# Feed forward products of a two-block transformer on block matrices: seven block products in place of eight for gate with up, and for the down projection of 16 of 22 f tiles

## The chip, the core and the metric

The kernel runs on one core of a Trainium2 chip. The metric is the device time of one execution in microseconds. A core has five engines with instruction queues of their own: TensorE (PE in the rows; its weight loads are PEld), VectorE (DVE), ScalarE (ACT), GpSimd (POOL) and SyncE (SP), which here issues nearly all DMA transfers. SBUF and PSUM are the memories on the core, each of 128 partitions; matmuls write PSUM alone, in banks of 128 x 512 float32 values.

## What is computed

Two transformer blocks follow each other on 512 tokens of width 1024, in float32. Each block has attention, or a mixer, and then a gated feed forward, with D_FF = 2816 = 22 tiles of 128. The change concerns the feed forwards alone:

```python
h = rms_norm(x, norm_ffn_pre[l])                                              # first block
f = (jax.nn.silu(h @ w_gate[l]) * (h @ w_up[l])) @ w_down[l]
x = x + rms_norm(f, norm_ffn_post[l])
...
h = rms_norm_2(x, norm_ffn[i])                                                # second block
x = x + (jax.nn.silu(h @ w_ffn_gate[i]) * (h @ w_ffn_up[i])) @ w_ffn_down[i]
```

## The kernel before, in words

**Precision.** Every large product is made of three matmuls (`mm3`, L136): a float32 operand is kept as a high part, rounded to float32r by ScalarE, and a low part, the rest, made by VectorE (or POOL). The products are high x high, high x low and low x high, summed in one PSUM bank. `load_w` (L123) loads 128 x 1024 weights by SyncE into a `raw` buffer (L131), ScalarE writes the high part (L132), `pl["lo"]` the low part (L133), into a `wt` buffer. `split_from` (L222) does the same for values on the core (L225, L226). Low parts of this kind read two operands from SBUF.

**The feed forward** (`ffn`, L664, called at L724 and L1022) goes over the 22 f tiles in three runs, 6, 8 and 8 (`SPLITS`). For each f tile `glu` (L653) makes gate and up with `t_mm` (L195): the weights stand in TensorE, all 512 tokens of the transposed input `hT` move, 8 k tiles x 3 matmuls for each. In the first run the first four tiles (`NFIRST`) are made in two halves of 256 tokens, so that the work begins when half of the tokens are ready. ScalarE makes the silu (L660), VectorE multiplies with up from PSUM (L661), and the result is split: high part on ScalarE (L225), low part on POOL (L226). Then the run's down products, `n_mm` (L202): for each of four token tiles two banks of 512 columns. VectorE adds them to a running result (L707, L709; L1011 in the second block), and after the last run the norms and transposes for the next part follow (`evac1`, `evac2`). All low parts of weights are VectorE's in these runs; eight weights of the head are POOL's.

**Before it**, in the first block, `norm_fill` (L589) makes the norm of a token tile and `tr_fill` (L596) transposes it (`transpose_tile`, L169); tiles 2 and 3 are made as late as inside the feed forward. In the second block the input comes tile by tile from the output projection.

**What sets the order.** The tile framework places instructions by priority and data, puts the semaphores in, and takes buffers from pools: 21 buffers `u`, two `raw`, four `wt1` and more `wt` in a phase, and eight PSUM banks (three `acc`, two `f`, one `av`, two `tp`). A load waits until its buffer is free, and engines work through their queues in order.

## Time and profile before

| | us |
|---|---|
| median of 3 runs | 1373.46 (1372.19 to 1374.2) |
| the profiled execution | 1375.31 |
| its span, first to last instruction | 1373.5 |
| TensorE busy | 1324.0 (96%) |
| VectorE busy | 715.1 (52%) |
| ScalarE busy | 595.1 (43%) |
| POOL busy | 250.2 (18%) |
| mean granted TensorE clock | 0.988 of full |

The page gives busy time of each engine, the span in 40 slices, the chain of work that ended last, groups of equal instructions and DMA issues. Ends of matmuls are modelled, so the distance from start to start tells their pace, not their listed duration. A duration on VectorE or POOL holds what the instruction waited for inside the engine; waits for semaphores are listed as idle time before it.

### The profile page before, as it was taken

The numbers are of one execution on the slowest core, as the hardware profiler recorded it, in microseconds if no ns is written. First come the engines' busy times: TensorE is split into PE (matmuls) and PEld (weight loads), VectorE is DVE, ScalarE is ACT, GpSimd is POOL, SyncE is SP. The second block draws the span as 40 slices with busy tenths as digits, with TensorE's granted clock in tenths as the row PEclk, the third lists the DMA queues.
The fourth block names the chain that finished last, engine by engine and source line by source line (L and its number), as shares of the span: only waits on it lengthen the run. The fifth ranks groups of instructions, "written<-read, shape, count | busy, mean of one in ns | idle before, by whom it ended". The sixth has DMA issues, their size and how long they took to land.

```text
span 1373.5 us, 17214 instructions
## 1 busy us (share of the span) xinstructions
PE 1324.0 (96%) x6476; PEld 1080.8 (79%) x6476; DVE 715.1 (52%) x1399; ACT 595.1 (43%) x1087; POOL 250.2 (18%) x255
## 2 busy tenths in 40 slices
PE   8889998899999999999999999989999999999997
PEld 6656666798888888878777778879988888888886
DVE  5889677742433242386886672655423321422464
ACT  5578876340322132244866564524413220422252
POOL 1433234320111011100323010115210110021002
PEclk9999999899999999999999999999999999999999
DMA  7212123241533143223121435634424330532031
GB/s 271 92 31 78 47 74 111 93 138 47 153 92 107 39 146 98 71 93 100 63 77 54 130 132 192 198 108 143 134 77 121 95 106 17 160 115 93 1 108 62
DMA packets 44771, 139.64 MB, mean 102 GB/s; under 512 B 7312, under 2 KB 7696, under 8 KB 44688
## 3 DMA queue, kind: packets, MB, share of 16 engines
q1 hardware_dynamic: 44544, 138.54, 31.8%
q8 instruction: 51, 0.84, 0.2%
q14 instruction: 32, 0.26, 0.1%
q10 hardware_dynamic: 144, 0.00, 0.0%
HBM read 130.14 MB, written 8.39 MB: 101 GB/s over the span
## 4 chain that ended last, share of the span: by engine, by line
PE 76%; DVE 9%; issue 7%; ACT 3%; POOL 2%; DMA 1%; POOLq 0%; ACTq 0%; DVEq 0%
PE acc L139 10%; PE acc L140 10%; PE acc L138 10%; PE f L140 10%; PE f L138 10%; PE f L139 10%; PE av L139 3%; PE av L138 3%; PE av L140 3%; DVE wt L133 2%; PE av L475 1%; DVE p L858 1%; PE tp L468 1%; DMA raw<-in_w_out 1%; PE tp L175 1%
## 5 line engine op out<-in xcount | busy, mean ns | idle before, releaser
L133 DVE TENSOR_TENSOR wt<-raw,wt 128x1024 fp32r<-128x1024 f32 (+1 forms) x204 | 254.2, 1247 | 280.8 <-ACT wt L132 279.8
L132 ACT ACTIVATE wt<-raw 128x1024 fp32r<-128x1024 f32 (+1 forms) x220 | 231.3, 1056 | 352.4 <-issue 84.2
L138 PE MATMUL f<-u,wt 128*128 128x512 f32 (+1 forms) x556 | 210.8, 379 | 4.3 <-DVE u L575 4.1
L139 PE MATMUL f<-u,wt 128*128 128x512 f32 (+1 forms) x556 | 210.0, 378 | 0.2 <-DVE u L218 0.2
L140 PE MATMUL f<-u,wt 128*128 128x512 f32 (+1 forms) x556 | 209.6, 377 | 0.0
L226 POOL TENSOR_TENSOR u<-t,u 128x512 fp32r<-128x512 f32 (+1 forms) x52 | 82.1, 1580 | 541.0 <-ACT u L225 541.0
L139 PE MATMUL acc<-u,wt 128*128 128x512 f32 (+1 forms) x432 | 155.0, 359 | 0.0
L138 PE MATMUL acc<-u,wt 128*128 128x512 f32 (+1 forms) x432 | 154.9, 359 | 0.0
L140 PE MATMUL acc<-u,wt 128*128 128x512 f32 (+1 forms) x432 | 154.8, 358 | 0.0
L138 PEld LDWEIGHTS f<-u,wt 128*128 128x128 f32 x556 | 106.3, 191 | 23.1 <-DVE u L575 4.3
L138 PE MATMUL f<-wt,u 128*128 128x512 f32 x302 | 120.6, 399 | 2.1 <-ACT u L225 2.1
L140 PE MATMUL f<-wt,u 128*128 128x512 f32 x302 | 119.9, 397 | 1.4 <-DVE u L226 1.4
L139 PEld LDWEIGHTS f<-u,wt 128*128 128x128 f32 x556 | 106.4, 191 | 17.1 <-DVE u L218 0.4
L140 PEld LDWEIGHTS f<-u,wt 128*128 128x128 f32 x556 | 106.4, 191 | 16.9
L139 PE MATMUL f<-wt,u 128*128 128x512 f32 x302 | 119.4, 396 | 0.0
L138 PE MATMUL acc<-wt,u 128*128 128x512 f32 (+1 forms) x288 | 112.7, 391 | 5.9 <-ACT wt L132 5.9
L139 PE MATMUL acc<-wt,u 128*128 128x512 f32 (+1 forms) x288 | 112.8, 392 | 1.6 <-DVE wt L133 1.5
L140 PE MATMUL acc<-wt,u 128*128 128x512 f32 (+1 forms) x288 | 112.4, 390 | 0.0
L138 PEld LDWEIGHTS acc<-u,wt 128*128 128x128 f32 x432 | 82.2, 190 | 12.0
L140 PEld LDWEIGHTS acc<-u,wt 128*128 128x128 f32 x432 | 82.0, 190 | 11.9
L139 PEld LDWEIGHTS acc<-u,wt 128*128 128x128 f32 x432 | 82.0, 190 | 11.8
L661 DVE TENSOR_TENSOR t<-t,acc 128x512 f32<-128x512 f32 (+1 forms) x52 | 31.4, 604 | 94.4 <-PE acc L140 91.3
(257 smaller groups left out, 2138.0 us busy)
## 6 DMA issues: line engine op xcount, KB each, us to landing
raw<-in_w_out SPq DMA_DIRECT2D x24, 512.0 KB, 3.7
raw<-in_w_gate SPq DMA_DIRECT2D x22, 512.0 KB, 3.6
raw<-in_w_up SPq DMA_DIRECT2D x22, 512.0 KB, 3.6
raw<-in_w_down SPq DMA_DIRECT2D x22, 512.0 KB, 3.6
raw<-in_w_ffn_gate SPq DMA_DIRECT2D x22, 512.0 KB, 3.5
raw<-in_w_ffn_up SPq DMA_DIRECT2D x22, 512.0 KB, 3.5
raw<-in_w_ffn_down SPq DMA_DIRECT2D x22, 512.0 KB, 3.5
raw<-in_w_in SPq DMA_DIRECT2D x11, 512.0 KB, 5.5
```

Of the source, the lines that this page charges most:

```text
L132: nc.scalar.activation(w[:, 0, c], raw[:, c], AF.Copy)
L133: pl["lo"].tensor_tensor(w[:, 1, c], raw[:, c], w[:, 0, c].bitcast(F32), op=ALU.subtract)
L138: nc.tensor.matmul(ps, lhsT=st[0], rhs=mv[0], start=first, stop=False)
L139: nc.tensor.matmul(ps, lhsT=st[0], rhs=mv[1], start=False, stop=False)
L140: nc.tensor.matmul(ps, lhsT=st[1], rhs=mv[0], start=False, stop=last)
L175: nc.tensor.transpose(pt[:, j * P:(j + 1) * P], h_t[:, k * P:(k + 1) * P], ident)
L226: (lo_eng or nc.vector).tensor_tensor(lo, src, hi.bitcast(F32), op=ALU.subtract)
L468: nc.tensor.transpose(pt[:, c:c + P], pn[j][:, kc * P:(kc + 1) * P], ident)
L475: nc.tensor.matmul(o[s * 64:s * 64 + 64], lhsT=VT[kc][:, kv], rhs=ts[s][:, i * 256:i * 256 + 256], start=kc == 0, stop=kc == NT - 1, skip_ ...
L661: nc.vector.tensor_tensor(s[:, :n], s[:, :n], pu[:, :n], op=ALU.mult)
L858: nc.vector.tensor_tensor_scan(c[:, n - 1::-1], ones.to_broadcast([P, n]) if nq == 1 else restart[:, :n], e[:, n - 1::-1], 0.0, op0=ALU.mu ...
```

## The change

A matrix product of 2 x 2 blocks is made with seven block products, of sums and differences of the blocks, in place of eight.

*Gate and up together.* The left matrix is h, cut into two halves of 256 tokens and two of 512 inputs; the right one is [gate, up] of an f tile, cut the same way by inputs. The seven left blocks (`a11`, `a12`, `a22`, `p1`, `s2`, `s3`, `p4`) are made once by transposing h and differences of its halves (`left_raw`, `left_rest`). The right ones are the raw blocks and four sums for each f tile (`sums`), made by POOL from the raw weights and split by ScalarE and VectorE. Each of the seven products (`prod`) has 4 k tiles x 3 matmuls of 256 columns. VectorE combines them out of PSUM (`glu`).

*Down* for f tiles 0 to 15, in four groups of four: `down_left` makes the left blocks by POOL subtractions, `down_weights` the sums of two pairs of weight tiles, `down7` seven products of 12 matmuls of 512 columns and the sums onto the running result, by VectorE and POOL. The last six f tiles are done as before.

*Around it.* The head makes the gate's two raw products of six f tiles (`glu_head`, `NFIRST = 6`), whose raw weights are loaded again for the sums. Raw weights come through three buffers, split weights through five `wt` buffers and `u`, sums through three `e` buffers. x of the first block is written to memory before the feed forward and read again after it. Down weights lie as 22 tiles of 128 x 1024.

```diff
-NFIRST = 4
+NFIRST = 6
...
+    def sums(b11, b12, b21, b22):
+        e = pl["e"]
+        ta, tb = (e.tile([P, 2, 512], F32, tag="e", name=nm("e")) for _ in range(2))
+        add = nc.gpsimd.tensor_tensor
+        add(ta[:, 0], b11, b12, op=ALU.add)
+        add(tb[:, 0], ta[:, 0], b22, op=ALU.add)
+        add(tb[:, 1], b12, b22, op=ALU.add)
+        wb = w8(flat(tb))
+        add(ta[:, 1], tb[:, 0], b21, op=ALU.add)
+        wa = w8(flat(ta))
+        return wb, wa
...
+    def left_rest(X, h0, h1, j):
+        c1, c2 = u_tile([P, 2, 512]), u_tile([P, 2, 512])
+        sub = nc.vector.tensor_tensor
+        sub(c1[:, 0], h1[:, 0:512], h1[:, 512:1024], op=ALU.subtract)
+        sub(c1[:, 1], h0[:, 0:512], c1[:, 0], op=ALU.subtract)
+        left_block(X, "s2", c1[:, 1], j)
+        sub(c2[:, 0], h0[:, 0:512], h1[:, 0:512], op=ALU.subtract)
+        left_block(X, "s3", c2[:, 0], j)
+        left_block(X, "p1", c1[:, 0], j)
+        left_block(X, "a22", h1[:, 512:1024], j)
+        sub(c2[:, 1], h0[:, 512:1024], c1[:, 1], op=ALU.subtract)
+        left_block(X, "p4", c2[:, 1], j)
...
+    def glu_head(X, E, wg, f):
+        G = load_raw(wg[f])
+        w = w8(G)
+        ps = any8()
+        prod(ps, w, 0, X["a11"], True)
+        nc.scalar.activation(E[:, 0], ps[:, :256], AF.Copy)
+        prod(ps, w, 512, X["a12"], False)
+        silu(E[:, 2], ps[:, :256])
+    def glu(X, E, wg, wu, f, dst):
+        h = slice(0, 256)
+        tt = nc.vector.tensor_tensor
+        G, Uw = load_raw(wg[f]), load_raw(wu[f])
+        head = E is not None
+        if not head:
+            E = pl["ee"].tile([P, 4, 256], F32, tag="ee", name=nm("ee"))
+            wG = w8(G)
+        wb, wa = sums(G[:, 0:512], Uw[:, 0:512], G[:, 512:1024], Uw[:, 512:1024])
+        w22 = w4(Uw[:, 512:1024])
+        if not head:
+            pp = any8()
+            prod(pp, wG, 0, X["a11"], True)
+            nc.scalar.activation(E[:, 0], pp[:, h], AF.Copy)
+        up = t_tile([P, 2, 256])
+        pn = any8()
+        prod(pn, wb, 0, X["s2"], True)
+        tt(E[:, 1], pn[:, h], E[:, 0], op=ALU.subtract)
+        pq = any8()
+        prod(pq, wb, 512, X["s3"], True)
+        tt(up[:, 1], E[:, 1], pq[:, h], op=ALU.subtract)
+        pr = any8()
+        prod(pr, wa, 0, X["p1"], True)
+        tt(up[:, 1], pr[:, h], up[:, 1], op=ALU.add)
+        prod(pq, wa, 512, X["a22"], False)
+        tt(E[:, 3], pq[:, h], E[:, 1], op=ALU.subtract)
+        silu(E[:, 3], E[:, 3])
+        if not head:
+            prod(pp, wG, 512, X["a12"], False)
+            silu(E[:, 2], pp[:, h])
+        prod(pr, w22, 0, X["p4"], False)
+        tt(up[:, 0], pr[:, h], E[:, 1], op=ALU.add)
+        tt(dst, E[:, 2:4].rearrange("p a b -> p (a b)"), flat(up), op=ALU.mult)
...
+    def down_left(ra, last):
+        rb = u_tile([P, 4, 256])
+        sub = nc.gpsimd.tensor_tensor
+        sub(rb[:, 0], ra[:, 1], ra[:, 3], op=ALU.subtract)
+        sub(rb[:, 1], ra[:, 0], rb[:, 0], op=ALU.subtract)
+        sub(rb[:, 2], ra[:, 0], ra[:, 1], op=ALU.subtract)
+        sub(rb[:, 3], ra[:, 2], rb[:, 1], op=ALU.subtract)
+        T = [u_tile([P, 2, 2, 256], F32R) for _ in range(3)]
+        t0 = last if last is not None else u_tile([P, 2, 2, 256], F32R)
+        i0 = 0 if last is None else 1
+        split_from(ra[:, 0], t0[:, 0, i0], t0[:, 1, i0])
+        for t, src in ((T[0], flat(ra[:, 2:4])), (T[1], flat(rb[:, 0:2])), (T[2], flat(rb[:, 2:4]))):
...
+    def down_weights(wdown, f1, f2):
+        K1, K2 = load_raw(wdown[f1]), load_raw(wdown[f2])
+        w11 = w4(K1[:, 0:512])
+        wb, wa = sums(K1[:, 0:512], K1[:, 512:1024], K2[:, 0:512], K2[:, 512:1024])
+        return dict(b11=(w11, 0), t2=(wb, 0), t3=(wb, 512), t1=(wa, 0), t4=(wa, 512)), K2
...
+    def down7(wdown, fs, left, acc, fresh):
+        n = len(left)
+        W, K2 = zip(*[down_weights(wdown, fs[i], fs[n + i]) for i in range(n)])
+        tt = nc.vector.tensor_tensor
+        pt = nc.gpsimd.tensor_tensor
+        lo, hi = slice(0, 512), slice(512, 1024)
+        def product(banks, x, b, first):
+            for j in range(2):
+                for i in range(n):
+                    t, a = left[i][x]
+                    w, off = W[i][b]
+                    st = (t[:, 0, a, j * P:(j + 1) * P], t[:, 1, a, j * P:(j + 1) * P])
+                    mv = wcols(w, off, off + 512)
+                    for m, (u, v) in enumerate(((0, 0), (0, 1), (1, 0))):
+                        nc.tensor.matmul(banks[j], lhsT=st[u], rhs=mv[v], start=first and i == 0 and m == 0,
+                                         stop=i == n - 1 and m == 2, skip_group_check=True)
...
+        bq = [any8() for _ in range(2)]
+        product(bq, "s3", "t3", True)
+        wv = [t_tile([P, 512]) for _ in range(2)]
+        for j in range(2):
+            tt(wv[j], v[j], bq[j], op=ALU.subtract)
+            if not fresh:
+                pt(acc[2 + j][:, hi], acc[2 + j][:, hi], wv[j], op=ALU.add)
+                pt(acc[2 + j][:, lo], acc[2 + j][:, lo], v[j], op=ALU.subtract)
+                pt(acc[j][:, hi], acc[j][:, hi], v[j], op=ALU.add)
...
+        for i in range(n):
+            w2 = w8(K2[i])
+            W[i].update(b21=(w2, 0), b22=(w2, 512))
...
+        for n in GROUPS:
+            fs, left, last = list(range(f0, f0 + n)), [], None
+            for i in range(n // 2):
+                ra = u_tile([P, 4, 256])
+                for half, f in ((0, fs[i]), (1, fs[n // 2 + i])):
+                    glu(X, heads.get(f), wgate, wup, f, flat(ra[:, 2 * half:2 * half + 2]))
+                    if i == 0 and half == 0:
+                        release()
+                last, names = down_left(ra, last if i % 2 else None)
+                left.append(names)
+            held.append((fs, left))
+            f0 += n
...
-    def glu(hT, wg, wu, gt, halves):
-        for c0, c1 in halves:
-            n = c1 - c0
-            pg, pu = any_tile(), any_tile()
-            t_mm(pg, wg, 0, hT, c0, c1)
-            t_mm(pu, wu, 0, hT, c0, c1)
-            s = t_tile([P, S])
-            silus.append(nc.scalar.activation(s[:, :n], pg[:, :n], AF.Silu))
-            nc.vector.tensor_tensor(s[:, :n], s[:, :n], pu[:, :n], op=ALU.mult)
-            split_from(s[:, :n], gt[:, 0, c0:c1], gt[:, 1, c0:c1], lo_eng=nc.gpsimd)
```

What stands in the queues, in two places of the first feed forward.

POOL, f tiles 6 to 13, of the kernel before (`u` the split product, `t` the product):

```order
L226 TENSOR_TENSOR u_3686<-t_3754,u_3686 128x512
L226 TENSOR_TENSOR u_3687<-t_3819,u_3687 128x512
L226 TENSOR_TENSOR u_3688<-t_3884,u_3688 128x512
L226 TENSOR_TENSOR u_3689<-t_3949,u_3689 128x512
L226 TENSOR_TENSOR u_3690<-t_4014,u_3690 128x512
L226 TENSOR_TENSOR u_3691<-t_4079,u_3691 128x512
L226 TENSOR_TENSOR u_3692<-t_4144,u_3692 128x512
L226 TENSOR_TENSOR u_3693<-t_4209,u_3693 128x512
```

and of the changed kernel, from the sums of f tile 8 to those of the first down weights (`e` a sum, `raw` a raw weight, `u` left blocks of the down products):

```order
L270 TENSOR_TENSOR e_4148<-raw_4140,raw_4142 128x512
L272 TENSOR_TENSOR e_4149<-raw_4142 128x512
L271 TENSOR_TENSOR e_4149<-e_4148,raw_4142 128x512
L274 TENSOR_TENSOR e_4148<-e_4149,raw_4140 128x512
L385 TENSOR_TENSOR u_4123<-u_3911 128x256
L270 TENSOR_TENSOR e_4268<-raw_4261 128x512
L272 TENSOR_TENSOR e_4269<-raw_4261,raw_4263 128x512
L271 TENSOR_TENSOR e_4269<-e_4268,raw_4263 128x512
L274 TENSOR_TENSOR e_4268<-e_4269,raw_4263 128x512
L383 TENSOR_TENSOR u_4123<-u_3911 128x256
L384 TENSOR_TENSOR u_4123<-u_3911,u_4123 128x256
L386 TENSOR_TENSOR u_4123<-u_3911,u_4123 128x256
```

In the place of one low part for each f tile stand four additions, and subtractions and the sums of down weights among them.

VectorE, from f tile 14 on, of the kernel before (`wt` a weight's low part, `t` the product with up):

```order
L709 TENSOR_TENSOR u_3683<-acc_4435,u_3683 128x512
L133 TENSOR_TENSOR wt_4606<-raw_4605,wt_4606 128x1024
L133 TENSOR_TENSOR wt_4666<-raw_4665,wt_4666 128x1024
L133 TENSOR_TENSOR wt_4671<-raw_4670,wt_4671 128x1024
L661 TENSOR_TENSOR t_4530<-t_4530,acc_4481 128x512
L133 TENSOR_TENSOR wt_4731<-raw_4730,wt_4731 128x1024
L133 TENSOR_TENSOR wt_4736<-raw_4735,wt_4736 128x1024
L133 TENSOR_TENSOR wt_4796<-raw_4795,wt_4796 128x1024
L661 TENSOR_TENSOR t_4595<-t_4595,acc_4546 128x512
L133 TENSOR_TENSOR wt_4801<-raw_4800,wt_4801 128x1024
L133 TENSOR_TENSOR wt_4861<-raw_4860,wt_4861 128x1024
```

and of the changed kernel, about the end of f tile 7 (`ee` and `t` partial results, tiles from `acc`, `tp`, `av` in PSUM):

```order
L377 TENSOR_TENSOR u_3911<-ee_4006,t_4039 128x512
L226 TENSOR_TENSOR wt_4273<-e_4269,wt_4273 128x1024
L226 TENSOR_TENSOR wt_4277<-e_4268,wt_4277 128x1024
L226 TENSOR_TENSOR u_4128<-u_3911,u_4128 128x512
L226 TENSOR_TENSOR u_4129<-u_4123,u_4129 128x512
L226 TENSOR_TENSOR u_4130<-u_4123,u_4130 128x512
L226 TENSOR_TENSOR u_4160<-raw_4142,u_4160 128x512
L362 TENSOR_TENSOR ee_4144<-acc_4178,ee_4144 128x256
L365 TENSOR_TENSOR t_4177<-ee_4144,tp_4192 128x256
L368 TENSOR_TENSOR t_4177<-acc_4206,t_4177 128x256
L370 TENSOR_TENSOR ee_4144<-tp_4192,ee_4144 128x256
L376 TENSOR_TENSOR t_4177<-acc_4206,ee_4144 128x256
```

Low parts of weights stood between single products; now three low parts, the combinations that wait for TensorE's products, and the splits of left blocks follow each other in one queue.

## Rows read from the trace of the kernel before

**Rows 1.** The page: span, busy time of each engine, shares of the last chain.
```profile
span 1373.5 us, 17214 instructions
PE 1324.0 (96%) x6476; PEld 1080.8 (79%) x6476; DVE 715.1 (52%) x1399; ACT 595.1 (43%) x1087; POOL 250.2 (18%) x255
...
PE 76%; DVE 9%; issue 7%; ACT 3%; POOL 2%; DMA 1%; POOLq 0%; ACTq 0%; DVEq 0%
```

**Rows 2.** Windows of 100 us: length, busy us of each engine, clock, DMA.
```profile
300.00:400.00 100.00, 100.00 (x443) 82.80 (x442) 34.45 (x34) 27.96 (x33) 10.35 (x6) 1.00 0.34 103
400.00:500.00 100.00, 100.00 (x443) 82.81 (x442) 31.44 (x31) 23.21 (x27) 8.53 (x5) 1.00 0.30 91
1000.00:1100.00 100.00, 100.00 (x443) 82.68 (x442) 31.55 (x32) 25.29 (x30) 10.87 (x6) 1.00 0.32 99
1100.00:1200.00 100.00, 100.00 (x443) 82.81 (x442) 31.41 (x32) 24.23 (x29) 8.51 (x5) 1.00 0.30 91
```

**Rows 3.** Timeline, TensorE, first feed forward: start, us, engine, line, operation.
```profile
329.70 0.39 PE L140 MATMUL acc<-wt,u 128*128 128x512 f32 x1
...
374.12 0.39 PE L138 MATMUL f<-u,wt 128*128 128x512 f32 x1
```

**Rows 4.** Timeline, TensorE: first row of each stage, first after it.
```profile
231.22 0.28 PE L138 MATMUL acc<-u,wt 128*128 128x256 f32 x1
...
611.92 0.39 PE L138 MATMUL f<-wt,u 128*128 128x512 f32 x1
...
944.20 0.36 PE L138 MATMUL f<-u,wt 128*128 128x256 f32 x1
...
1308.64 0.27 PE L175 MATMUL tp<-ident,u 128*128 128x128 f32 x1
```

**Rows 5.** Timeline, TensorE, start of the second feed forward.
```profile
943.41 1.03 PE L175 MATMUL tp<-ident,u 128*128 128x128 f32 x8
...
944.40 0.28 PE L139 MATMUL f<-u,wt 128*128 128x256 f32 x1
...
946.20 0.28 PE L139 MATMUL f<-u,wt 128*128 128x256 f32 x1
```

**Rows 6.** Groups on POOL: shapes, count | busy us, mean ns | idle before.
```profile
L1052 POOL TENSOR_TENSOR u<-u,row 128x512 f32<-128x512 f32 x7 | 9.0, 1292 | 87.1 <-DVE u L1050 82.9 <-issue 4.2
L1052 POOL TENSOR_TENSOR u<-u,row 128x256 f32<-128x256 f32 x2 | 1.5, 734 | 2.9 <-DVE u L1050 2.9
```

**Rows 7.** Timeline, VectorE and POOL where they meet, and POOL alone (405.07).
```profile
361.50 1.23 DVE L133 TENSOR_TENSOR wt<-raw,wt 128x1024 fp32r<-128x1024 f32 x1 [0.70 <-ACT wt L132]
362.07 1.82 POOL L226 TENSOR_TENSOR u<-t,u 128x512 fp32r<-128x512 f32 x1 [42.75 <-ACT u L225]
...
405.07 1.28 POOL L226 TENSOR_TENSOR u<-t,u 128x512 fp32r<-128x512 f32 x1 [8.86 <-ACT u L225]
...
893.56 1.29 POOL L970 TENSOR_TENSOR t<-t,u 128x512 f32<-128x512 f32 x1 [2.77 <-ACT t L967]
893.85 2.08 DVE L133 TENSOR_TENSOR wt<-raw,wt 128x1024 fp32r<-128x1024 f32 x1
...
935.75 2.44 DVE L155 SCALAR_TENSOR_TENSOR rs_t<-rs_y,rs_a 128x1 f32<-128x1 f32 x1
935.76 4.75 POOL L133 TENSOR_TENSOR wt<-raw,wt 128x1024 fp32r<-128x1024 f32 x2 [29.78 <-ACT wt L132]
938.31 2.22 DVE L159 SCALAR_TENSOR_TENSOR rs_y<-rs_t,rs_y 128x1 f32<-128x1 f32 x1
...
942.89 2.40 POOL L133 TENSOR_TENSOR wt<-raw,wt 128x1024 fp32r<-128x1024 f32 x1 [2.38 <-DMA u<-spill_x]
943.05 0.69 DVE L988 TENSOR_TENSOR u<-f,u 128x512 f32<-128x512 f32 x1 [0.99 <-DMA u<-spill_x]
943.66 0.68 DVE L988 TENSOR_TENSOR u<-acc,u 128x512 f32<-128x512 f32 x1
```

**Rows 8.** Groups on VectorE by shape: two SBUF inputs, and one from PSUM (L661).
```profile
L317 DVE TENSOR_TENSOR t<-t,t 128x512 f32<-128x512 f32 x8 | 5.5, 687 | 1.2 <-POOL t L314 1.0
L420 DVE TENSOR_TENSOR sq<-sq,sq 128x256 f32<-128x256 f32 x10 | 4.6, 460 | 1.4 <-ACT sq L417 1.4
L661 DVE TENSOR_TENSOR t<-t,acc 128x256 f32<-128x256 f32 x16 | 6.7, 417 | 12.6 <-PE acc L140 9.6 <-ACT t L660 2.9
```

**Rows 9.** Timeline, VectorE: the last step of the norms in the first stage.
```profile
262.87 1.89 DVE L1070 SCALAR_TENSOR_TENSOR u<-x,rs_y,row 128x512 f32<-128x512 f32 x2
```

**Rows 10.** The page, DMA issues: transfers, KB each, us to landing.
```profile
raw<-in_w_up SPq DMA_DIRECT2D x22, 512.0 KB, 3.6
```

**Rows 11.** Groups on ScalarE: the high parts.
```profile
L132 ACT ACTIVATE wt<-raw 128x1024 fp32r<-128x1024 f32 x217 | 229.5, 1062 | 351.9 <-issue 84.2 <-PE f L140 70.9 <-PE acc L140 49.2
L225 ACT ACTIVATE u<-t 128x512 fp32r<-128x512 f32 x48 | 29.8, 620 | 22.3 <-DVE t L661 15.0 <-DVE t L974 6.5 <-DVE t L777 0.8
```

274 lines of the change are left out of this document (188 added, 86 removed).

## The prediction

> **What bounds the kernel now.** I read the busy shares first, then the 100 us windows, then the order of single matmuls, and only then the other engines. TensorE is busy for 96% of the span and carries 76% of the chain that ended last [rows 1]. In the four windows that lie inside the two feed forwards it is busy for 100.00 of 100 us, while VectorE and POOL are busy for about 31 to 34 and 9 to 11 us [rows 2]. "Busy" alone would not prove that it works at its pace, so I took start to start: 196 matmuls of 512 columns between 329.70 and 374.12 us are 0.2266 us each, without a hole [rows 3]. So in these stretches time is a number of matmuls times their pace, and everything else is hidden. A change that takes matmuls away there gives time back at once, up to the point at which another resource needs longer than what is left.
>
> Extents: the first feed forward runs from 231.22 to 611.92 us, 380.7 us; the second from 944.20 to 1308.64 us, 364.4 us [rows 4]. The work of one: 384 matmuls of 256 columns and 1392 of 512. A 256 column matmul comes every 0.120 us (944.40 to 946.20 us, 15 steps), eight transposes take 0.79 us (943.41 to 944.20), 0.1 us each [rows 5]. 384 x 0.120 + 1392 x 0.2266 + 32 x 0.1 = 46.1 + 315.4 + 3.2 = 364.7 us. The second stage fits this within 0.5 us; the first has 16 us of waits on top, at its start.
>
> **What TensorE saves.** Gate and up of one f tile were 48 matmuls of 512 columns (10.88 us) or 96 of 256 (11.52). Now they are 7 products x 4 x 3 = 84 of 256 columns, 84 x 0.120 = 10.08 us. The seven-eighths is not seen in full, since two halves cost 0.240 where one whole costs 0.2266. Down: four f tiles were 96 matmuls of 512 columns, now 84, 19.03 us; four groups 76.1 us, and the last six tiles as before, 144 x 0.2266 = 32.6. Transposes: 14 blocks x 4 = 56, 5.6 us. Sum: 221.8 + 76.1 + 32.6 + 5.6 = 336.1 us for each feed forward, 28.6 less, 57.2 for both. If all else stays hidden, that is the gain.
>
> The Trainium skill ("TensorE: Matmul & The Clock Gate", Back-to-back issue gap) gives 262 cycles for a 256 column matmul, an estimate of 0.109 us at 2.4 GHz. The row here says 0.120; by the page gate and up would be 40 us cheaper over both stages, and the measurement decides.
>
> **What is added, and where it lies.** Each gate and up tile now needs two more weight blocks that are sums. Per f tile POOL makes four additions of 128x512, and VectorE writes the low parts: three of 128x1024 (wG, wb, wa; two where the head has made wG), one of 128x512 for w22, one product of 128x512 at the end. A down group of four f tiles adds two times four POOL additions, eight POOL subtractions of 128x256 and six POOL additions of 128x512 onto the running result (not in the first group of the first stage), and on VectorE six low parts of 128x1024, eight of 128x512 and two of 128x256. In return POOL loses its old low parts of this stage.
>
> Durations. POOL, two SBUF inputs: 512 columns 1.28 to 1.29 us, 256 columns 0.73 [rows 6, 7]. VectorE, two SBUF inputs: 1024 columns 1.23 [rows 7], 512 columns 0.69, 256 columns 0.46 [rows 8]. Added up by engine this looks harmless: a steady f tile is 4 x 1.29 = 5.2 us on POOL, 3 x 1.23 + 2 x 0.69 = 5.1 us of such work on VectorE, each about half of TensorE's 10.08.
>
> The rows say that the two halves do not overlap. The low part of a weight starts on VectorE at 361.50 and takes 1.23 us; POOL's operation starts at 362.07 and takes 1.82, not the 1.28 of the undisturbed one at 405.07: it ends 2.39 us after VectorE's start, against 1.23 + 1.29 = 2.52 for one after the other [rows 7]. In the other direction, POOL at 893.56 for 1.29, VectorE's low part from 893.85 takes 2.08 and ends 1.08 us after POOL did, 0.15 less than its own 1.23. At 935.75 a VectorE instruction on one element per partition takes 2.44 us, as long as POOL's, and another the same way at 938.31. VectorE's two additions at 943.05 and 943.66, with one input in PSUM, run 0.69 and 0.68 in the middle of a POOL operation [rows 7]. So an operation of POOL and a VectorE operation with two SBUF inputs exclude each other, and each hand over saves 0.13 to 0.15 us of the sum. I call this shared time. It is a resource of its own, which the page does not list.
>
> The Trainium skill ("SBUF — State Buffer", Who interferes with whom) states this as an exclusive lock on a shared port pair that is held for a whole instruction and leaves out VectorE instructions with one SBUF input. The trace agrees with both (1.82 against 1.28, 0.69 undisturbed). The rule speaks against this change, and without it the sum would end at the first rival below.
>
> Shared time of one feed forward, second stage: POOL 144 x 1.29 + 32 x 0.73 = 209.1 us; VectorE 94 x 1.23 + 94 x 0.69 + 8 x 0.46 = 184.2 us; together 393 us. Of VectorE's, the 94 long ones are 6 + 16 + 44 + 24 + 4 (heads, wG, wb and wa, down, last six), the 94 short ones 22 + 22 + 32 + 8 + 10 (w22, products, down, the subtractions of the left blocks, last six). The first stage has six POOL additions less, 386 us. The lower bound lets each of the 176 (170) POOL operations alternate with VectorE, 0.28 us saved at each: 344 and 338 us. The upper bound saves nothing.
>
> Where can this lie? Not beside the last 32.6 us of down products, whose weights are ready, and hardly beside the head (six first halves of the gate, 6 x 24 x 0.120 = 17.3 us, and the transposes, 5.6), which asks for 13 us of it. So a stage takes (shared time - 13) + 22.9 + 32.6 us. Second stage: 387 to 436 us, against 364.4. First stage: 381 to 429, plus about 12 us at its start: there the left blocks need the norm of all tokens. Its last step ends at 264.76 us, 33.5 us after the stage began [rows 9]; some 8 us of that are waits behind POOL's low parts as at 938.31, which go, and the head's six low parts add 7. The left blocks follow, and the head covers 22.9 us where two runs of half-width matmuls covered 46. So 393 to 441, against 380.7. In a steady group of four the same is seen in small: TensorE 40.3 + 19.0 = 59.4 us, shared time 4 x 10.2 + 38 = 79 us plain, 68 with every hand over saved.
>
> I take the middle for both, 411 and 417: the hand overs are partly saved, but the shared time has also holes, since VectorE works in order and its low parts of the next weights stand behind operations that wait for TensorE, and POOL waits for a raw weight (3.6 us from issue to landing [rows 10], with three buffers in a ring). +47 and +36 make +83 us. ScalarE's high parts (94 x 1.06 + 94 x 0.62 us [rows 11], 158 of some 410 us) stay hidden, and so does the spill of x. The profiled execution took 1375.31 us with a span of 1373.5, the median is 1373.46; the overhead outside the span is the same after. 1373.46 + 83 = **1457 us** (rounded up).
>
> **Rivals.**
> 1. Faster: the shared time is hidden after all. For it: TensorE is the only bound in the four windows, POOL is idle for 90%, and each engine's own sum per f tile (5.2, and 5.1 plus five PSUM reads of 0.42 [rows 8], 7.2 us) is under 10.08. Then 1373.5 - 57.2 + 12 = 1328, between 1316 and 1345. It decides from the point at which a group's shared time falls under TensorE's 59.4; it would have to be 13% below my lowest price. Against it: each of the rows 7.
> 2. Slower yet: shared time and landing times add up in a chain instead of overlapping. Thirty times in a stage the sums wait for a raw buffer that the sums before set free: 3.6 + 4 x 1.29 + one low part 1.23 = 10.0 us, no slack under 10.08. If each round loses another 0.7 to 2.4 us by this, that is 21 to 72 for each stage on top: 1500 to 1600. For it: three raw buffers, five weight buffers. Against it: VectorE can use the holes.
> 3. Shared time at its lowest and some of it moved beside the last down products or before the stage: 387 - 13 and 393 - 13: +10 and 0, so 1383 at the least, to 1408; a little under it if the first stage's start costs nothing new.
>
> **How the numbers follow.** My forecast, 1408 to 1505 (bounds of the two stages, 387 + 393 to 436 + 441, against 745): 0.68. Rival 1: 0.12. Rival 2: 0.12, a half of it taken under 1530. Rival 3: 0.08. The range from 1390 to 1530 leaves out rival 1, the half of rival 2 above it and a little of rival 3: 0.2. About 0.2% is what a measurement can tell from no change: within it 0.02, from rival 3's lower end. Faster 0.12, slower 0.86.
>
> **What would show it.** TensorE busy falls from 100 to about 75 to 88 us per 100 in the windows inside a feed forward, with matmuls waiting for VectorE's or ScalarE's parts of wb and wa. Mean durations rise: POOL's additions above 1.29, VectorE's long low parts above 1.26, towards 1.8. The 256 column matmuls keep 0.120 us where they run in a row, else the TensorE term is wrong. Gate and up alone run near 10 to 10.6 us per f tile; the loss lies around the down groups. If VectorE's and POOL's means stay at 1.26 and 1.3 and TensorE has no holes, rival 1 is right and the exclusion was read too strictly; if SyncE's loads end most of the waits, it is rival 2.

## The result

The changed kernel takes 1633.21 us in the median (1630.64 to 1635.85, 4 runs), the kernel before 1373.83 beside it: a ratio of 1.1889, 95% interval 1.1865 to 1.1913. The prediction named the direction, but 1633 lies far above its range of 1390 to 1530. 176 us of the loss have to be explained on top of the 83 that were forecast.

The page of the changed kernel, same lines as [rows 1]:

```profile
span 1632.4 us, 20842 instructions
PE 1379.5 (85%) x7628; PEld 1164.8 (71%) x7628; DVE 1073.0 (66%) x1897; ACT 738.0 (45%) x1325; POOL 612.6 (38%) x533
```

No engine is full any more. The timeline of TensorE tells where the two feed forwards begin and end (first product of each, last matmul of the first, first transpose after the second), as [rows 4] did:

```profile
230.19 1.09 PE L328 MATMUL f<-u,wt 128*128 128x256 f32 x7
...
719.96 0.39 PE L140 MATMUL acc<-u,u 128*128 128x512 f32 x1
...
1071.97 0.55 PE L328 MATMUL f<-u,wt 128*128 128x256 f32 x2 [2.96 <-ACT wt L225]
...
1556.46 1.04 PE L175 MATMUL tp<-ident,u 128*128 128x128 f32 x8
```

The windows view of exactly these two stretches (columns as in [rows 2]: length, busy us of each engine, granted clock):

```profile
230.19:720.19 490.00, 389.55 (x2385) 351.43 (x2384) 324.06 (x495) 183.55 (x297) 236.46 (x173) 0.90 0.26 84
1071.97:1556.46 484.49, 390.01 (x2384) 351.57 (x2385) 313.11 (x438) 175.81 (x284) 246.02 (x176) 0.90 0.25 79
```

490.0 us against 380.7 and 484.5 against 364.4: +109.3 and +120.1. The rest went from 628.4 to 657.9 us, +29.5: 1.0 less before the first stage, 19.5 more between the two, 11.1 more behind the second. Inside the stretches TensorE was 100.00% busy [rows 2]; now it is 80%, VectorE 65 to 66%, POOL 48 to 51%. The groups on POOL and VectorE (count, busy us, mean ns, idle time before and what ended it):

```profile
L271 POOL TENSOR_TENSOR e<-e,raw 128x512 f32<-128x512 f32 x60 | 90.0, 1500 | 41.3 <-DMA raw<-in_w_ffn_down 20.4 <-DMA raw<-in_w_down 19.4 <-DVE t L368 1.5
L274 POOL TENSOR_TENSOR e<-e,raw 128x512 f32<-128x512 f32 x60 | 81.2, 1354 | 3.1
L272 POOL TENSOR_TENSOR e<-raw 128x512 f32<-128x512 f32 x44 | 70.3, 1598 | 0.0
L270 POOL TENSOR_TENSOR e<-raw,raw 128x512 f32<-128x512 f32 x44 | 63.5, 1443 | 289.5 <-DMA raw<-in_w_ffn_up 106.2 <-DMA raw<-in_w_up 60.5 <-DVE u L1320 40.4
...
L226 DVE TENSOR_TENSOR wt<-e,wt 128x1024 fp32r<-128x1024 f32 x120 | 164.1, 1371 | 166.0 <-ACT wt L225 165.7
...
L226 DVE TENSOR_TENSOR wt<-raw,wt 128x1024 fp32r<-128x1024 f32 x68 | 102.4, 1512 | 15.0 <-ACT wt L225 15.0
```

Lines 270 to 274 are the four sums of a weight, in the order 270, then 271 and 272, then 274. They take 1.35 to 1.60 us where an undisturbed one takes 1.29 [rows 6], and the low parts 1.37 and 1.51 us against 1.23 [rows 7]. So the exclusion is there. But POOL also stands idle, waiting for raw weights that have not landed, and the list of waits (us in all, times, longest) shows a chain through four engines:

```profile
ACT wt L225 <- POOL e L271: 201.6, 44, 8.3
DVE wt L226 <- ACT wt L225: 180.6, 66, 6.9
...
POOL e L270 <- DMA raw<-in_w_ffn_up: 106.2, 8, 69.5
...
PE tp L328 <- DVE t L365: 72.7, 26, 5.8
```

ScalarE waits for the sum, VectorE for ScalarE, TensorE for VectorE, POOL for the load (the 69.5 us at once end at 1088.60, and 53 of them lie ahead of the second stage). Counting every instant in which an operation of POOL or one of VectorE with two inputs from SBUF ran, the shared time used is 383 us in the first stage and 373 in the second (each instant once, from the trace). In 107 and 112 us neither ran.

### The profile page after: what moved, and what is told of

Same layout as the page of the kernel before. It is cut to its first block, busy times and chain, and to the rows that moved or that the text cites. A ratio compares the mean times of both kernels' runs of the same rounds, so it can differ in the third digit from the quotient of the medians.

```text
span 1632.4 us, 20842 instructions
## 1 busy us (share of the span) xinstructions
PE 1379.5 (85%) x7628; PEld 1164.8 (71%) x7628; DVE 1073.0 (66%) x1897; ACT 738.0 (45%) x1325; POOL 612.6 (38%) x533
## 5 line engine op out<-in xcount | busy, mean ns | idle before, releaser
L226 DVE TENSOR_TENSOR wt<-e,wt 128x1024 fp32r<-128x1024 f32 x120 | 164.1, 1371 | 166.0 <-ACT wt L225 165.7
L328 PE MATMUL tp<-sh,wt 128*128 128x256 f32 x912 | 147.1, 317 | 83.6 <-DVE t L365 72.7
L328 PEld LDWEIGHTS tp<-sh,wt 128*128 128x128 f32 x912 | 134.5, 221 | 90.7 <-DVE t L365 78.2
L133 DVE TENSOR_TENSOR wt<-raw,wt 128x1024 fp32r<-128x1024 f32 (+1 forms) x88 | 108.6, 1237 | 55.3 <-ACT wt L132 54.6
L328 PE MATMUL f<-u,wt 128*128 128x256 f32 x816 | 127.9, 310 | 12.1 <-ACT ee L358 5.6
L328 PEld LDWEIGHTS f<-u,wt 128*128 128x128 f32 x816 | 120.1, 220 | 15.0 <-ACT ee L358 6.0
L138 PE MATMUL f<-u,wt 128*128 128x512 f32 x272 | 108.3, 398 | 0.3 <-ACT nx L998 0.2
L139 PE MATMUL f<-u,wt 128*128 128x512 f32 x272 | 107.4, 395 | 0.0
L140 PE MATMUL f<-u,wt 128*128 128x512 f32 x272 | 107.3, 395 | 0.0
L132 ACT ACTIVATE wt<-raw 128x1024 fp32r<-128x1024 f32 (+1 forms) x88 | 91.5, 1047 | 32.9 <-PE f L140 12.5
L271 POOL TENSOR_TENSOR e<-e,raw 128x512 f32<-128x512 f32 x60 | 90.0, 1500 | 41.3 <-DMA raw<-in_w_ffn_down 20.4
L138 PE MATMUL f<-wt,u 128*128 128x512 f32 (+1 forms) x208 | 83.7, 406 | 4.6 <-ACT wt L132 4.3
L139 PE MATMUL f<-wt,u 128*128 128x512 f32 (+1 forms) x208 | 83.6, 403 | 1.9 <-DVE rs_y L150 1.4
L140 PE MATMUL f<-wt,u 128*128 128x512 f32 (+1 forms) x208 | 83.7, 403 | 0.0
L274 POOL TENSOR_TENSOR e<-e,raw 128x512 f32<-128x512 f32 x60 | 81.2, 1354 | 3.1
```

Of the source, the lines that this page charges most:

```text
L132: nc.scalar.activation(w[:, 0, c], raw[:, c], AF.Copy)
L133: pl["lo"].tensor_tensor(w[:, 1, c], raw[:, c], w[:, 0, c].bitcast(F32), op=ALU.subtract)
L138: nc.tensor.matmul(ps, lhsT=st[0], rhs=mv[0], start=first, stop=False)
L139: nc.tensor.matmul(ps, lhsT=st[0], rhs=mv[1], start=False, stop=False)
L140: nc.tensor.matmul(ps, lhsT=st[1], rhs=mv[0], start=False, stop=last)
L226: (lo_eng or nc.vector).tensor_tensor(lo, src, hi.bitcast(F32), op=ALU.subtract)
```

## The experiments

Unless said otherwise, a number for a stage is the time from the start of its first product of gate and up to that of its last: 453.9 and 449.5 us in the changed kernel, of which TensorE needs 302 at its pace. A stage that an edit left alone came out up to 8 us different, so smaller differences are not read.

### One half of the change at a time

The down projection with eight products, in four runs as the last six f tiles of the changed kernel are done (`gateup_only`):

```diff
+        runs = (6, 6, 6, 4)
...
-        for n in GROUPS:
...
+        for n in runs:
...
+                glu(X, heads.get(f), wgate, wup, f, g)
+                if f == f0 and held:
+                    down(*held.pop(), False)
```

> Seven products for gate with up in all 22 f tiles, and the down projection with eight, in four runs of 6, 6, 6 and 4 f tiles. TensorE per feed forward: 221.8 + 22 x 24 x 0.2266 + 5.6 = 347 us, 17.7 less than before. Shared time per feed forward 22 x 10.2 = 225 us, far under it. Theory A (shared time alone is the bound; the changed kernel's holes come from VectorE and POOL excluding each other): all of it lies beside TensorE, 1373.8 - 35 and up to 30 for what the changed kernel lost outside the feed forwards: 1338 to 1370. Theory B (each round of sums waits for a raw weight that a late low part frees, three raw buffers, and this adds up with the work behind it): the f tiles of the changed kernel that have no down group beside them took 10 to 18 us from one product to the next, 13 in the mean, against 10.1; 22 x 2.5 us come back per feed forward: 1440 to 1490.

Measured: 1525.41 us, ratio 1.1112 (1.1096 to 1.1129). Both theories were too low (1338 to 1370 and 1440 to 1490), and the idea that the shared time alone decides is out: in 404.1 to 467.7 us it is used for 42 of 64 us, yet the f tiles come every 12.7 us. One round on SyncE (transfers issued), POOL and VectorE, from the timeline:

```profile
402.66 0.33 SPq L246 DMA_DIRECT2D raw<-in_w_gate  x1
...
416.45 0.33 SPq L246 DMA_DIRECT2D raw<-in_w_up  x1
420.58 0.33 SPq L246 DMA_DIRECT2D raw<-in_w_gate  x1
...
410.29 1.28 POOL L270 TENSOR_TENSOR e<-raw,raw 128x512 f32<-128x512 f32 x1 [7.65 <-DVE ee L370]
411.53 2.27 POOL L272 TENSOR_TENSOR e<-raw 128x512 f32<-128x512 f32 x1
413.76 1.29 POOL L271 TENSOR_TENSOR e<-e,raw 128x512 f32<-128x512 f32 x1
415.13 1.29 POOL L274 TENSOR_TENSOR e<-e,raw 128x512 f32<-128x512 f32 x1
424.44 1.29 POOL L270 TENSOR_TENSOR e<-raw,raw 128x512 f32<-128x512 f32 x1 [8.01 <-DMA raw<-in_w_gate]
...
416.18 1.33 DVE L226 TENSOR_TENSOR wt<-e,wt 128x1024 fp32r<-128x1024 f32 x1 [3.53 <-ACT wt L225]
...
417.87 0.69 DVE L377 TENSOR_TENSOR t<-ee,t 128x512 f32<-128x512 f32 x1
...
419.87 0.68 DVE L226 TENSOR_TENSOR u<-raw,u 128x512 fp32r<-128x512 f32 x1
```

The last sum ends at 416.42, and 0.03 us later the load that wanted its raw buffer is issued. The next gate is issued at 420.58, when VectorE has made the low part of w22 (419.87 to 420.55), which is the last reader of its buffer. That weight lands, and the first sum of the next round starts at 424.44, 14.15 us after the first sum of this one. Of these 6.1 are the four sums (one stretched to 2.27, beside VectorE), 8.0 waiting. This closes the loop: w22's low part stands in VectorE's queue behind the product that ends the f tile before (417.87), that one behind the low part of a sum (416.18), and this one had waited 3.53 us for ScalarE, which had waited for POOL's sum.

Seven products for down alone (`down_only`):

```diff
+    def glu(hT, w, dst, c0, c1):
...
+        t_mm(pg, w[0], 0, hT, c0, c1)
+        t_mm(pu, w[1], 0, hT, c0, c1)
+        silus.append(nc.scalar.activation(s[:, :n], pg[:, :n], AF.Silu))
+        nc.vector.tensor_tensor(dst[:, c0:c1], s[:, :n], pu[:, :n], op=ALU.mult)
```

> Gate and up with eight products as before (one matmul of 512 columns for each step, the first two f tiles in halves), the down projection of 16 f tiles with seven. TensorE per feed forward: 22 x 10.88 + 76.1 + 32.6 + 3.2 = 351 us, 14 less than before. Shared time per feed forward: 44 low parts x 1.23 + 4 groups x 38 + about 15 = 221 us. Theory A: hidden, 1373.8 - 28 and up to 30 for what was lost outside: 1346 to 1376. Theory B: the second weight tile of each pair holds its raw buffer until the last products of the group, one raw buffer is left for the next gate and up, and a group loses the 15 to 20 us that a group of the changed kernel loses over its f tiles: 8 x 15 to 20 on top, 1465 to 1510.

Measured: 1423.84 us, ratio 1.0377 (1.0359 to 1.0394), between the two. TensorE runs at its pace except in the down groups and at the stages' ends. Start to start against the pace, three of the four groups of a stage lose 5 to 9 us each (the expectation of down_wide, below, says 2 to 7), the fourth nothing. In a group (SyncE's transfers, POOL, TensorE):

```profile
440.40 0.33 SPq L246 DMA_DIRECT2D raw<-in_w_down  x1
...
444.06 1.28 POOL L271 TENSOR_TENSOR e<-e,raw 128x512 f32<-128x512 f32 x1 [3.12 <-ACT t L391]
...
447.73 0.50 PE L384 MATMUL f<-wt,sh 128*128 128x512 f32 x1 [1.36 <-ACT wt L225]
```

The fourth weight of the group is asked for at 440.40, when the group's products already run (from 438.78). It lands at 443.92, 0.14 us ahead of the sum at 444.06 (whose row names an operation of ScalarE that ends at the same time): the raw ring again, which `down_wide` below tests.

### The sums: left out, without loads, on VectorE

All three are edits of `sums`. `no_sums` splits raw weights in place of sums, `const_sums` adds blocks of the transposed input, `sums_dve` changes the engine:

```diff
-        add(ta[:, 0], b11, b12, op=ALU.add)
...
-        wa = w8(flat(ta))
-        return wb, wa
+        return w8(b12), w8(b22)
```

```diff
+        x = pl["stand"]
+        b11, b12, b21, b22 = (x[i // 2].rearrange("p a b c -> p (a b c)")[:, i % 2 * 512:i % 2 * 512 + 512].bitcast(F32)
+                              for i in range(4))
```

```diff
-        add = nc.gpsimd.tensor_tensor
+        add = nc.vector.tensor_tensor
```

> The changed kernel with POOL's sums of weights left out (the low and high parts are made of raw weights in their place, so the outputs are not the reference's). VectorE's low parts, TensorE's products and the loads stay. POOL keeps the subtractions and the additions onto the running result. Shared time per feed forward: 184 of VectorE and about 55 of POOL. Theory A: hidden, TensorE's 336 us decide, 1316 to 1375. Theory B: raw weights are free earlier, since 5.2 us of sums leave the chain of 10 us, but the second down weights still hold two of three raw buffers: 1400 to 1500. A third theory, C: after each wait TensorE is granted half its clock for a while, and this alone makes the excess over the forecast (about 300 of 1848 short matmuls per feed forward came every 0.20 us or more); then it goes with the waits, whichever cause they have.

> The changed kernel with the same number and shapes of POOL's sums, but of blocks that lie in memory all the time (the transposed input) in place of the raw weights, so the outputs are not the reference's. The sums wait for no load and hold no raw buffer. Shared time is unchanged, 375 to 395 us per feed forward. Theory A: 1600 to 1640, nothing gained. Theory B: what is left is the shared time, and the forecast of 1457 (1408 to 1505) is met. Theory C goes with the waits.

> The changed kernel with the sums of weights made by VectorE in place of POOL, the same additions of 128x512 (0.69 us there, 1.29 on POOL). Shared time of a group of four f tiles falls from 79 to 64 us plain, VectorE's own time rises to 69 (with its reads of PSUM); TensorE's stays 59.4. Theory A (shared time decides): a group comes down from 87 by 12 to 17 us, 8 groups and the 12 last f tiles: 1490 to 1540. Theory B (landing and the chain behind it decide, const_sums gave 79 us back): each round has 4 x 0.6 us less in its chain, 60 rounds: 1490 to 1560 as well, but VectorE then makes the sums behind its other work in one queue, where they wait for a landing and hold up everything behind them: up to 1640.

| kernel | us | first stage | second stage |
|---|---|---|---|
| changed kernel | 1633.2 | 453.9 | 449.5 |
| no_sums | 1409.8 | 339.4 | 341.3 |
| const_sums | 1554.1 | 420.5 | 407.3 |
| sums_dve | 1507.4 | 390.4 | 388.6 |

(no_sums and const_sums are one execution each.) The sums cost 223 us. Waiting for their loads, and holding raw buffers meanwhile, is 79 of it; the same additions on VectorE, where each takes 0.68 to 0.70 us and no second engine has to be waited for, cost 126 less. Even without sums the kernel is 36 us above before. Of the theories, no_sums falls into the band of B, const_sums between A and B, and sums_dve into both.

### Two edits that did not test what they were meant to

`early_w22` splits w22 ahead of the sums, `raw_u4` puts a buffer `u` into the ring:

```diff
+        w22 = w4(Uw[:, 512:1024])
         wb, wa = sums(G[:, 0:512], Uw[:, 0:512], G[:, 512:1024], Uw[:, 512:1024])
-        w22 = w4(Uw[:, 512:1024])
```

```diff
-        pl["raws"] = [rawp] * 2 + [pl["raw2"]]
+        pl["raws"] = [rawp] * 2 + [pl["raw2"]] + [up] * 1
```

> One line of the changed kernel moved: the last block of up (w22) is split before the sums of its f tile instead of behind them. Nothing is added or left out. In the trace this split ended about 9 us after its weight had landed, since ScalarE made the high parts of the sums ahead of it and VectorE the product of the f tile before, and the load of the f tile after waits for it. Theory A: no change, 1615 to 1650. Theory B: the next load starts some 3 to 8 us earlier, an f tile without a down group comes at 11 us in place of 13: 1560 to 1610.

> The changed kernel with a fourth raw buffer in the ring, which is taken from the 21 buffers u that the left blocks, partial results and small splits share. Theory A: no change or worse (one u less), 1615 to 1660. Theory B: the rounds overlap with the landings, most of the 79 us that sums without loads gave back: 1550 to 1600.

early_w22: 1633.16 us, as the changed kernel. In its trace the split still stands late in ScalarE's and VectorE's queues (in one f tile at 466.89 and 467.62, 5 us behind the end of the last sum at 461.63), so the edit did not move it and the run decides nothing. raw_u4: 1736.90 us. The fourth buffer made things worse. What grew are SyncE's waits for a low part that writes a `u` (us in all, times, longest; raw_u4, then the changed kernel):

```profile
SPq L247 <- DVE u L226: 500.5, 47, 19.7
```

```profile
SPq L246 <- DVE u L226: 88.5, 28, 8.6
```

All 47 stand ahead of a load into a buffer `raw`, and 45 of them end with a low part that had read such a buffer, as w22's does. The 36 loads into a buffer `u` themselves waited 25 us in all. So the raw buffers came free later, with one `u` less for everything else; why, no run shows, and raw_u4 is no test of the ring.

### Exclusion, buffers, ring

One input per operation on POOL (`sums_one`):

```diff
-        add(ta[:, 0], b11, b12, op=ALU.add)
...
+            nc.gpsimd.tensor_scalar(o, x, 1.0, 0.0, op0=ALU.mult, op1=ALU.add)
+            nc.gpsimd.tensor_scalar(o[:, 0:256], y[:, 0:256], 1.0, 0.0, op0=ALU.mult, op1=ALU.add)
```

> The changed kernel with each of POOL's sums replaced by two POOL operations that read one operand each, one of 512 columns (0.80 us in the trace of before) and one of 256 (about 0.5): the same time on POOL, the same weights waited for and held, the same buffers written, but no sum is made, so the outputs are not the reference's. Theory A (an operation of POOL and one of VectorE with two inputs from SBUF exclude each other, and this is most of the loss): VectorE's long low parts fall from 1.37 and 1.51 us to 1.23 to 1.26, and the 93 to 104 us per feed forward in which both were listed as busy at once come back for the most part: 1440 to 1540. Theory D (what costs is the way of a sum through POOL, 5 us for four in a row, before ScalarE and VectorE can begin; the exclusion only stretches rows that wait anyway): 1590 to 1640.

Measured: 1546.02 us, 87 less (stages 410.3 and 409.8), between the two bands. It does not tell the theories apart, because the exclusion did not go away (POOL's timeline, undisturbed rows and at 306.06 one beside VectorE; then VectorE's):

```profile
302.96 0.62 POOL L270 TENSOR_SCALAR e<-raw 128x512 f32<-128x512 f32 x1
...
305.69 0.41 POOL L271 TENSOR_SCALAR e<-raw 128x256 f32<-128x256 f32 x1
306.06 1.67 POOL L270 TENSOR_SCALAR e<-raw 128x512 f32<-128x512 f32 x1
...
306.02 1.23 DVE L226 TENSOR_TENSOR wt<-e,wt 128x1024 fp32r<-128x1024 f32 x1 [2.97 <-ACT wt L225]
```

0.62 us alone, 1.67 beside VectorE's low part: it ends 0.48 us after that one did. The Trainium skill ("SBUF — State Buffer", Who interferes with whom) says that a VectorE instruction with two SBUF inputs contends with any GpSimd instruction that reads SBUF; this row agrees. Each pair of operations is also 0.26 us shorter than a sum (0.62 + 0.41 against 1.29), 240 times, 62 us of POOL's time.

VectorE's low parts of the sums (wb and wa) made by ScalarE (`low_act`, first diff), the running result of the first stage in two buffers (`acc_half`), the two buffers won given to the raw ring (`raw_five`, the last line), and the last two on top of low_act and sums_dve (`low_five`, `dve_five`):

```diff
-            split_from(src, w[:, 0], w[:, 1])
+            nc.scalar.activation(w[:, 0], src, AF.Copy)
+            nc.scalar.activation(w[:, 1], src, AF.Copy)
```

```diff
-    acc1 = [u_tile([P, D]) for _ in range(NT)]
+    acc1 = [u_tile([P, D]) for _ in range(2)] * 2
+    pl["raws"] += [u_tile([P, D]) for _ in range(2)]
```

> The changed kernel, the low parts of the sums (wb and wa) made by ScalarE as a plain copy in place of VectorE's difference, so the outputs are not the reference's. POOL makes all its sums as before, and a sum's way to TensorE is as long: ScalarE's 1.06 us in place of VectorE's 1.23. Of VectorE's operations with two inputs from SBUF 60 long ones per feed forward are gone, 74 us of shared time. Theory A (exclusion): POOL's sums fall from means of 1.37 to 1.55 us towards 1.29, and the time by most of 2 x 74 us: 1490 to 1550. Theory D (the length of the way through POOL alone): 1600 to 1640, and slower where ScalarE's 64 us more per feed forward are in the way.

> The changed kernel with the running result of the first feed forward in two buffers u in place of four: the token tiles 2 and 3 are added onto those of 0 and 1, so the outputs are not the reference's, and two more of the 21 buffers are free there. The second feed forward is unchanged and serves as the comparison within the run. raw_u4 took one u away and lost 104 us. Theory U (the buffers u are short by themselves: of 21, 8 are held all the time, and a down group with its 7 left blocks, 2 weights and 3 partial results leaves the next f tile one): the first feed forward falls from 490 to 440 to 475 us, the second stays at 484. Theory A: both stay within 5 us.

> acc_half (the running result of the first feed forward in two buffers, so the outputs are not the reference's; by itself it left both stages where they were) with the two buffers that this sets free used as a fourth and fifth raw buffer in the first feed forward. The second feed forward keeps three and is the comparison. Theory B (loop: the last sum of an f tile frees the raw weight that the next f tile's load needs, 3.6 us to land, then four sums of 5.2 to 6.1 us; about 10 us and more in each round): the first feed forward falls by what sums without loads gave there, 35 to 45 us, from 490 to 445 to 460; the second stays at 484. Theory A (exclusion alone): both stay within 5 us. Theory D (the way through POOL, without the landing): both stay within 10 us.

> low_act and raw_five together: the low parts of the sums copied by ScalarE, five raw buffers and the running result in two buffers in the first feed forward (the outputs are not the reference's); the second has three raw buffers as low_act. From the first product of gate and up to its last, the first feed forward took 454 us in the changed kernel, 436 in low_act (18 less), 425 in raw_five (28 less), 339 with the sums left out. If the shared time and the ring of raw buffers are two bounds of nearly one length, each of which hid what the other's removal was worth, both together give far more than 46: 340 to 385 us. If their effects add up, 400 to 415, and what is left is the way of the sums through POOL (theory D).

> sums_dve with five raw buffers and the running result in two buffers in the first feed forward (outputs not the reference's there); the second stays as in sums_dve. Sums on VectorE gave 390 us from first to last product of gate and up. If landings are what is left between that and TensorE's 302: 335 to 360. If VectorE's own queue is (336 us listed as busy of the 390): 365 to 390.

| kernel | us | first stage | second stage |
|---|---|---|---|
| low_act | 1589.4 | 435.7 | 424.9 |
| acc_half | 1628.6 | 453.2 | 449.0 |
| raw_five | 1602.4 | 425.5 | 448.7 (three raw buffers) |
| low_five | 1546.1 | 391.9 | 429.2 (three raw buffers) |
| dve_five | 1484.5 | 376.3 | 380.4 (three raw buffers) |

low_act took 120 low parts of 1.23 us, 148 us of shared time, away and got 44 back, between the bands of the two theories, and POOL's sums hardly became shorter: of the second stage, low_act (first row) and the changed kernel:

```profile
L275 POOL TENSOR_TENSOR e<-e,raw 128x512 f32<-128x512 f32 x30 | 45.4, 1515 | 25.4 <-DMA raw<-in_w_ffn_down 25.2
```

```profile
L271 POOL TENSOR_TENSOR e<-e,raw 128x512 f32<-128x512 f32 x30 | 46.5, 1551 | 21.9 <-DMA raw<-in_w_ffn_down 20.4 <-DVE t L368 1.5
```

acc_half moved nothing: the buffers `u` are not short by themselves, and theory U falls. raw_five is the clean test of the ring. Its first stage loses 28 us against acc_half, its second nothing, less than the 35 to 45 expected and more than the exclusion or POOL's way alone allowed. Both removed at once give 62 us (low_five), more than 18 + 28 and less than the 70 to 115 that two bounds hiding each other would have given. So in the first stage the sums cost 115 us (453.9 - 339.4): ring and the low parts of the sums 62; the remaining 53, a difference and not a measurement, are left for the way of four sums through POOL. How much of these 53 is POOL's own length, and how much its stretching beside VectorE's other operations, no run separates. In dve_five the two buffers are worth 14 us in the first stage, where the second, which they leave alone, differs by 8 as well; 376.3 lies in the band in which VectorE's own queue decides.

The same contrast without down groups, `gateup_dve` (gateup_only with `add = nc.vector.tensor_tensor`):

> gateup_only with the sums made by VectorE. An f tile is 10.0 us of VectorE's work (3 low parts, 4 sums of 0.69, w22, the product, its split, and the reads of PSUM) against TensorE's 10.08. gateup_only's f tiles came every 13.5 us although the shared time was used for only 42 of 64 us. If the way through POOL (four sums of 1.29 to 2.3 us between landing and ScalarE) makes the 13.5, f tiles come every 10 to 10.8 us: 1525 - 2 x 17 x 3 = 1410 to 1440. If the landing of raw weights in three buffers makes it: 13 us stay, 1500 to 1530.

Measured: 1412.55 us, 113 under gateup_only. The rows of the product that ends an f tile, six in a row, in gateup_only and in gateup_dve:

```profile
L377 DVE TENSOR_TENSOR t<-ee,t x6: 684/692/1775, 404.1 to 467.7; 128x512 f32<-128x512 f32 x6
```

```profile
L377 DVE TENSOR_TENSOR t<-ee,t x6: 681/683/686, 377.1 to 431.1; 128x512 f32<-128x512 f32 x6
```

Five steps in 63.6 us, 12.7 each, and in 54.0, 10.8 each, with the same raw ring. What made an f tile late was the way through POOL. With the sums on VectorE the same loads are nearly in time (in the second f tile shown VectorE waits 1.6 us for a gate, POOL had waited 8.0): the four sums take 2.4 us less even where nothing stretches them, no second engine is waited for, and POOL's part of the exclusion is gone. The edit does all three at once, and which of them counts most is not shown. TensorE's granted clock is 0.89 in the first of these two windows and 1.00 in the second.

### A form that is faster than both

`down_wide`: down_only with six raw buffers, and x read back into raw buffers that the weights loaded next do not use. `down_wide2`: besides, the first two weights are asked for ahead of the copy of x to memory, and the input of the last projection is loaded before the second feed forward, which has four raw buffers here.

```diff
-        phase(sh=10, raw2=1, wt=1, t=5, ee=1, e=3)
+        phase(sh=7, raw2=4, wt=1, t=5, e=3)
...
-        m, xt = acc1[tt], load_raw(spill["x1"][tt])
+        m, xt = acc1[tt], pl["raw2"].tile([P, D], F32, tag="raw", name=nm("raw"))
```

```diff
+    first = [(w8(load_raw(A["w_gate"][0])), w8(load_raw(A["w_up"][0])))]
...
-    ffn_phase()
+    ffn_phase(2, pT=2)
+    pT = []
```

> down_only (seven products for the down projection of 16 f tiles, gate and up as before) with six raw buffers for three, the memory taken from buffers that this form leaves empty, and x of the first block read back into raw buffers that the next stage does not load its weights into. In down_only TensorE lost 2 to 7 us in each down group, where the sums of the second pair waited for a late load (issued at 440.40, landed about 444 us, first product at 447.73), and about 30 us at the ends of the two feed forwards. If the raw ring is the cause of both: 1423.8 - 8 x 4 - 15 to 25, 1365 to 1380. If the down groups wait for the exclusion instead: 1395 to 1415.

> down_wide with two transfers moved: the weights of the first f tile are asked for ahead of the copy of x to memory, which waits for the norms in the same queue (TensorE lost about 6 us there against before), and the input of the last projection is loaded before the second feed forward and its products stand ahead of the last stage's change of buffers, as in before (9.5 us there). If these are the two places, 1375.5 - 10 to 16: 1358 to 1366, about 1% under before. If TensorE finds no other work there: no change.

down_wide: 1375.45 us, ratio 1.0018 (1.0007 to 1.0028); by the count that gave 5 to 9 us, the down groups now lose 0.4 to 0.5. down_wide2: 1364.80 us, ratio 0.9949 (0.9937 to 0.9961), faster than before by half a per cent. That is 8 us, where the matmuls left out are worth 28 by the sum in the expectation of down_only; where the rest goes is not shown. Its feed forwards (windows, columns as above) are TensorE's again, with POOL at 42 and 48%:

```profile
400.00:500.00 100.00, 100.00 (x441) 82.29 (x440) 56.89 (x62) 37.80 (x52) 41.82 (x35) 1.00 0.31 99
1100.00:1200.00 100.00, 100.00 (x441) 82.27 (x440) 59.55 (x64) 37.85 (x51) 48.15 (x37) 1.00 0.29 90
```

## Why the prediction was wrong, step by step

**Right.** TensorE's work, 336 us for each stage, fits: the matmuls that ran (1848 of 256 columns, 480 of 512 and 56 transposes in each) make 336.1 at their pace. The mean durations of sums and low parts rose as the exclusion demands. The shared time used, 383 and 373 us, lies inside its bounds (338 to 386 and 344 to 393), 21 and 4 us above the middle that was taken.

**Right by luck.** TensorE's busy share fell to 80, in the 75 to 88 named. But 336 of 490 us are 69%: the busy time listed is 390 us, 53 more than the pace explains, since it holds the matmuls at the lower clock (below) and the modelled ends. The share fits a stage of some 420 us, and the stages took 485 and 490.

**The step that failed: holes in the shared time.** The sum gave a stage its shared time plus 42.5 us (and 12 more at the first one's start) and nothing else. It knew of holes, but had them paid out of saved hand overs: even the top of its range has none inside the loop. In truth neither engine used it for 107 and 112 us, 52 and 69 more than assumed. With the 25 us of shared time above the middle this is 147 of the missing 176. It treated two queues that work in order, and that wait for each other in every round, as if they were one resource that is always fed. low_act shows the error in the other direction: taking 148 us from that resource gave only 44 back. In gateup_only, where the parts can be followed, a loop fills the holes: release, landing, sums on POOL, splits on ScalarE and VectorE, release.

**The rival that came true was priced too low.** Rival 2, the chain of landings and sums, had a chance of 0.12 and 21 to 72 us for each stage (its top, 1600, still lies under 1633), from a round of 10.0 us, "no slack". The 10.0 were 3.6 + 4 x 1.29 + 1.23, all undisturbed durations, in the same text that showed them stretching to 1.8. In gateup_only one round took 14.15 us: the sums 6.1, and 8.0 waiting, because the next gate's buffer was freed by w22's low part, which stood in VectorE's queue behind the last product of the f tile before. A round at 12.7 to 14 us does not fit under 10.08, and everything behind it shifts. The prediction put the loss around the down groups and gate and up at 10 to 10.6 us; gateup_only, with only that half of the change, is 152 us slower than before.

**What was taken as free.** 29.5 us lie outside the stages, where the sum had none ("so does the spill of x"). Between the stages TensorE waits, among others, 4.3 us for late weights: the first load of the next part is issued 4.7 us after the first stage's end (724.88), behind x read back and written out in SyncE's queue, and in before 4.2 us ahead of it (607.68). Behind the second stage TensorE stands 7.2 us, waiting for a norm; before had the products of the last projection to run there, and their input is now loaded only from 1557.29 on. In the smaller kernel, down_wide and down_wide2 mended both (that first load went from 624.00 in down_only to 573.15 in down_wide), and the copy of x out that stood ahead of the first weights in SyncE's queue. How the 29.5 divide in the changed kernel was not measured. The prediction put the spill at nothing without a reason, and not by the queue that it stands in.

**Rival 1** (all hidden) is refuted by the 1633 and the stretched durations; even with the sums taken out 1410 are left, against its 1316 to 1345. **Rival 3** did not occur.

## What to carry to other kernels

Work that "fits beside" a busy engine has to fit as a loop: follow one buffer from its release through landing, sum, split and product to its next release, with the stretched durations, and compare that with the time that the busy engine gives one round. Added up by engine, or by shared port, the parts are a lower bound only. And before sums are put on an idle engine, ask who waits for them: here the same additions on the busier VectorE were 126 us cheaper, where they take half as long and need no second queue.

## What the runs showed of the chip that was not expected

**The clock.** The granted clock was 1.00 in the four windows of before [rows 2] and 0.90 in both of the changed kernel. After a wait TensorE works at the lower of its two levels, 1.2 GHz, for a while (timeline of TensorE in the changed kernel):

```profile
409.74 2.23 PE L328 MATMUL f<-u,wt 128*128 128x256 f32 x10 [2.40 <-ACT ee L358]
411.77 2.37 PE L328 MATMUL tp<-sh,wt 128*128 128x256 f32 x12
```

Ten matmuls in 2.03 us, 0.203 each, where the pace is 0.120; the granted clock is 0.59 from 409.74 to 411.77. Over all starts, matmuls at this slower step cost some 40 us in each stage, a part of the holes that the prediction did not have. It goes with the waits: in no_sums, in 368.6 to 500.4 us, it is under 2 us. No run takes it away by itself, so whether it lengthens the loop, as VectorE's combinations wait for these matmuls, or only follows it stays open.

**POOL with one input.** An operation of POOL that reads one operand from SBUF is held up by VectorE's two-input operation just as one that reads two (0.62 and 1.67 us above).

**One queue for all loads.** A transfer that waits for its buffer or its data holds all that SyncE would issue after it: 500 us of waits for one kind of low part in raw_u4, and some 11 us at the two places that down_wide2 mended.
